# Residual stream parked in DRAM during the gate and up products, the final norm by halves of the tokens, and one mLSTM output projection placed earlier

## The chip, the cores and the metric

The kernel runs on one core of a Trainium2 chip. The metric is the device time of one execution in microseconds; the time of a kernel is the median of several executions. Within the kernel TensorE (PE) multiplies, PEld loads its weights, VectorE (DVE) and ScalarE (ACT) work on elements, GpSimd (POOL) does small work and issues accumulating transfers, and SyncE (SP) issues the other transfers in order.

## The reference

A trunk of two layers on 512 tokens with 1024 features, in float32:

```python
for layer in range(DEPTH):                       # DEPTH = 2
    x = x + 0.5 * swiglu(rmsnorm(x, ffn_norm[layer, 0]), ...)      # hidden size 2816
    h = rmsnorm(x, mix_norm[layer])
    y = mla(h, ...) if layer % 3 == 0 else mlstm(h, ...)           # 8 heads each
    x = x + y
    x = x + 0.5 * swiglu(rmsnorm(x, ffn_norm[layer, 1]), ...)
return rmsnorm(x, final_norm)
```

`swiglu` is `(silu(h @ w_gate) * (h @ w_up)) @ w_down`. So the phases are a gated block (f0), attention (a), two gated blocks (f1, f2), the matrix memory (m), a gated block (f3) and the final norm.

## The kernel before

**Data.** The residual x is kept transposed: eight tiles of 128 features by 512 tokens, in pairs, `xx[0]` to `xx[3]`, each 128x1024 float32 and in a pool of constants. All other large tiles (normed operands, activations, weights that are summed) come from one pool of 31 tiles of 128x1024 (`ARENA`, `duo`); plain weight pieces land in a pool of three (`wp`, tag `raw`).

**Products.** Every float32 product is three matmuls on operands split into a high and a low part: ACT casts the high part (`whi`, L162), DVE subtracts to get the low part (`wlo`, L163). A gated block does gate and up first: two plain pieces (`plain`, L411), then nine pieces by seven products instead of eight (`seven`, L433), 24 matmuls of 128x256 for each product. The operand combinations of the seven products are made from x by `normed_blocks` (L363). Down follows: `down_plain` (L507) and `down_seven` (L571), whose seven products end in additions into x (`add`, L599) and, for the next norm, squares of x on ACT that DVE sums (`square`, L261).

**Weights.** A list of planned pieces sets the order of the loads. SP issues them in that order (L122), four ahead of use; where two weight blocks have to be added, POOL issues the second as an accumulating transfer (L125, L167), or DVE adds (L150). An SP load into a buffer in use stands at the head of SP's queue until the buffer's last reader is done.

**The order of instructions** on each engine is fixed when the kernel is built, by a scheduler that goes by the order of the program and its own costs.

**mLSTM.** In `mlstm` (L947) the loop `for p in range(3)` (L1223) runs over pairs of heads. Per head, `conv` projects and convolves queries and keys, `gate` projects the output gate (`og`), `decay` makes the decay weights (spread of rows, exponentials on ACT into `dw`) and the scores `s`, `mix` multiplies scores and values (`num`) and sums rows (`rows`). `out(part, i)` is a piece of the output projection: 24 matmuls into `y` and two additions into x (L1265). In the last turn (p = 2) `out(0, 0)` stands behind `decay(6)`.

**Final norm.** `finish` (L1301) is called last: a sum over features by matmuls with ones (`st`, L273), the inverse root on POOL (L281), a spread over partitions by two matmuls with diagonal operands (`bc`, L292 and L296), then for each of the eight tiles of x one DVE instruction of 128x512 (L1306) and a transfer of 256 KB (L1308).

Of the kernel before, what the change touches and what calls it, by code (L numbers as in the profile page):

```python
# [34 lines left out]
P = 128  # L35
T = 512
# [6 lines left out]
NU = NF // 2  # L43
NB = 2
DC = 3
ARENA = 31
LOADS = 4
AHEAD = 2
WARM = 36
# [15 lines left out]
class Trunk:  # L65
    def __init__(self, ctx, tc, t, out):
        self.tc, self.nc, self.t, self.out = tc, tc.nc, t, out
        self.const = ctx.enter_context(tc.tile_pool(name="const", bufs=1))
        self.wp = ctx.enter_context(tc.tile_pool(name="wp", bufs=3))
        self.tmp = ctx.enter_context(tc.tile_pool(name="tmp", bufs=8))  # L70
        self.small = ctx.enter_context(tc.tile_pool(name="small", bufs=2))
        self.ps = ctx.enter_context(tc.tile_pool(name="ps", bufs=6, space=bass.MemoryType.PSUM))
        self.ps2 = ctx.enter_context(tc.tile_pool(name="ps2", bufs=2, space=bass.MemoryType.PSUM))
        self.arena = ctx.enter_context(tc.tile_pool(name="arena", bufs=ARENA))
        self.xx = [self.const.tile([P, 2, T], F32, name=f"xx{d}") for d in range(ND // 2)]
        self.x = [self.xx[d // 2][:, d % 2] for d in range(ND)]
        self.chunks, self.loads, self.loaded, self.split, self.made = [], [], [], [], {}
        self.first = 0

# [4 lines left out]
    def pair(self, name="pr"):  # L84
        d = self.duo(name)
        return d[:, :T], d[:, T:]

    def bank(self, name="mm"):
        return self.ps.tile([P, T], F32, name=name, tag="mm")
# [141 lines left out]
    def norm_begin(self, gcol):  # L231
        self.xg = [None] * ND
        self.gcol = gcol
        self.acc = self.small.tile([P, T], F32, name="acc", tag="acc", bufs=2)
        self.nacc = 0

    def norm_split(self, d):

# [1 line left out]
        self.split_to(self.xg[d], self.x[d], self.vec(self.gcol + d))  # L240

    def norm_square(self, d):
        self.square(self.acc, self.x[d], self.nacc == 0)
        self.nacc += 1

    def norm_tile(self, d):

# [4 lines left out]
    def norm_half(self, d, n):  # L252

        t = slice(n * T // 2, n * T // 2 + T // 2)
        if self.gcol is not None:
            if self.xg[d] is None:
                self.xg[d] = self.pair()
            self.split_to([a[:, t] for a in self.xg[d]], self.x[d][:, t], self.vec(self.gcol + d))
        self.square(self.acc[:, t], self.x[d][:, t], False)

    def square(self, acc, src, first):  # L261
        if first:
# [6 lines left out]
    def rstd(self, acc, n, times=None):  # L269

        st = self.ps2.tile([P, T], F32, name="st", tag="st")
        for q in range(NT):
            self.nc.tensor.matmul(st[:, q:q + 1], acc[:, q * P:(q + 1) * P], self.one, start=True, stop=True)  # L273
        ms = self.small.tile([P, NT], F32, name="ms", tag="ms")
        if times is not None:
            self.nc.vector.tensor_tensor(out=ms, in0=st[:, 0:NT], in1=times, op=ALU.mult)
            self.nc.vector.tensor_scalar(ms, ms, 1.0 / n, EPS, ALU.mult, ALU.add)
        else:
            self.nc.vector.tensor_scalar(ms, st[:, 0:NT], 1.0 / n, EPS, ALU.mult, ALU.add)
        r = self.small.tile([P, NT], F32, name="r", tag="r", bufs=6)  # L280
        self.nc.gpsimd.tensor_tensor(out=r, in0=ms, in1=self.mhalf[:, 0:NT], op=ALU.pow)  # L281
        return r

    def spread(self, r):

        hi = self.small.tile([P, NT], F32R, name="rh", tag="rh")
        lo = self.small.tile([P, NT], F32, name="rl", tag="rl")
        self.split_to((hi, lo), r)
        bc = self.ps2.tile([P, T], F32, name="bc", tag="st")
        for n, part in enumerate((hi.bitcast(F32), lo)):  # L290
            diag = self.tmp.tile([P, T], F32R, name="diag", tag="t")
            self.nc.vector.tensor_tensor(  # L292
                out=diag.rearrange("p (a b) -> p a b", a=NT),
                in0=self.ident[:, None, :].broadcast_to([P, NT, P]),
                in1=part[:, :, None].broadcast_to([P, NT, P]), op=ALU.mult)
            self.nc.tensor.matmul(bc, self.onesr, diag, start=n == 0, stop=n == 1)  # L296
        return bc

# [64 lines left out]
    def normed_blocks(self, rb):  # L363
# [35 lines left out]
        split(7, t3)  # L399
        yield  # L400
        b21 = block(1, 0)
        yield
        split(2, b21)
        yield
# [74 lines left out]
    def ffn(self, f, next_gain):  # L479
        v = self.nc.vector  # L480
        xg = self.xg
        self.gcol_now = self.gcol
        acts, slabs = [], []
        for j in range(NU):
            g, i = divmod(j - DC, 4)
            if j < DC:
                acts.append(self.duo("act", F32))
                outs = [acts[j][:, i * 256:i * 256 + 256] for i in range(4)]
            else:
                if i == 0:  # L490
                    slabs.append([self.duo("slab", F32) for _ in range(4)])
                outs = [a[:, i * 256:i * 256 + 256] for a in slabs[g]]
            if j < NB:
                for half in range(2):
                    self.plain(f, j, half, xg, acts[j][:, half * T:half * T + T])
            else:
                self.seven(outs)
            if i == 3 and j > DC:

                b11, b12, _, b22 = slabs[g]  # L500
                v.tensor_tensor(out=b12, in0=b22, in1=b12, op=ALU.subtract)
                v.tensor_tensor(out=b12, in0=b12, in1=b11, op=ALU.add)
        self.norm_begin(next_gain)
        self.down_plain(f, acts, self.operands(slabs))
        self.down_seven(slabs)
# [65 lines left out]
    def down_seven(self, slabs):  # L571
# [57 lines left out]
        for c in range(4):  # L629
            product(bw, 7, c, last=False)  # L630
            product(bx, 2, c)
        add(1, 1, bw, -0.5)
        add(0, 0, bx, 0.5)
        for d in range(4):
            self.norm_tile(d)
        for c in range(4):
            product(bw, 4, c, first=False)
            self.norm_half(4 + c, 1)
        add(1, 0, bw, -0.5)
        for d in range(4, 8):  # L640
            self.norm_half(d, 0)

    def plan_ffn(self, f):
        for j in range(NB):
# [302 lines left out]
    def mlstm(self, next_gain):  # L947
# [275 lines left out]
        for p in range(3):  # L1223
# [86 lines left out]
    def run(self, phases):  # L1310
        gains = {"f0": V_FFN, "f1": V_FFN + ND, "f2": V_FFN + 2 * ND, "f3": V_FFN + 3 * ND,
# [12 lines left out]
        for p, q in zip(phases, phases[1:] + ["end"]):  # L1324
# [3 lines left out]
                self.mla(gains[q])  # L1328
            else:
                self.mlstm(gains[q])  # L1330
        self.finish()

# [96 lines left out]
```

## Time and profile before

| | |
|---|---|
| median of 3 executions | 1866.14 us (1862.98 to 1870.06) |
| the profiled execution, its own time | 1857.42 us |
| its span in the trace | 1855.7 us |
| granted TensorE clock, mean of the span | 0.992 |
| PE busy | 1811.5 us (98%) |
| DVE, ACT, POOL busy | 79%, 50%, 7% |
| HBM read and written | 261.62 MB and 2.10 MB |

Durations in the trace belong to the profiled execution, which lies 8.7 us under the median. A row of a timeline gives the start in microseconds from the span's start, the duration, the engine, the line, the operation and, in brackets, how long the engine was idle before and what released it.

### The profile page before, as it was taken

How to read it: one execution, taken by the hardware profiler on the slowest of the kernel's cores; microseconds unless marked ns; L12 is line 12 of the kernel's file. 1: busy time of each engine (PE TensorE's matmuls, PEld its weight loads, DVE VectorE, ACT ScalarE, POOL GpSimd, SP SyncE). 2: the span in 40 equal slices, each digit the busy share in tenths (PEclk: the TensorE clock that was granted, in tenths of full speed). 3: DMA queues.
4: the chain of work that ended last, by engine and by line, in shares of the span. 5: the costliest groups of instructions: out<-in, count | busy, mean ns of one | idle time of the engine just before them, and what ended most of it. 6: DMA issues, size and time to landing. Idle time of an engine off the chain costs nothing.

```text
span 1855.7 us, 30086 instructions
## 1 busy us (share of the span) xinstructions
PE 1811.5 (98%) x12240; PEld 1662.8 (90%) x12240; DVE 1463.2 (79%) x1931; ACT 934.9 (50%) x1339; POOL 131.3 (7%) x154
## 2 busy tenths in 40 slices
PE   9999999999999999999999999999998999999996
PEld 7999989978887999989989999997876779999896
DVE  7877899777767877877796878778877778788875
ACT  5444545567544444544544444455757544445442
POOL 0010011000000010000001000100000000100010
PEclk9999999999999999999999999999998999999998
DMA  6683567421124684566377456733221246845662
GB/s 205 177 236 110 162 187 163 137 74 63 46 73 150 159 243 128 140 181 153 126 219 205 133 162 187 175 105 101 80 69 57 69 126 181 236 125 149 184 159 91
DMA packets 74906, 265.66 MB, mean 143 GB/s; under 512 B 8336, under 2 KB 9360, under 8 KB 74768
## 3 DMA queue, kind: packets, MB, share of 16 engines
q1 hardware_dynamic: 57312, 200.30, 30.9%
q0 software_dynamic: 17456, 63.44, 19.4%
q8 instruction: 96, 1.57, 0.3%
q14 instruction: 42, 0.34, 0.1%
HBM read 261.62 MB, written 2.10 MB: 142 GB/s over the span
## 4 chain that ended last, share of the span: by engine, by line
PE 73%; issue 13%; DVE 8%; ACT 3%; DMA 2%; POOL 0%; POOLq 0%; DVEq 0%; ACTq 0%
PE pz L450 4%; PE pw L449 4%; PE pw L448 4%; PE pz L449 4%; PE pz L448 4%; PE pw L450 3%; PE y L194 3%; PE y L196 3%; PE y L195 3%; PE px L449 3%; PE px L448 3%; PE px L450 3%; PE py L450 2%; DMA raw<-in_wgs 2%; PE py L448 2%
## 5 line engine op out<-in xcount | busy, mean ns | idle before, releaser
L162 ACT CAST whi<-raw 128x1024 fp32r<-128x1024 f32 (+1 forms) x278 | 284.9, 1025 | 412.2 <-issue 131.1
L163 DVE TENSOR_TENSOR wlo<-raw,whi 128x1024 fp32r<-128x1024 f32 (+1 forms) x278 | 330.5, 1190 | 109.1 <-ACT whi L162 108.1
L162 ACT CAST whi<-sum 128x1024 fp32r<-128x1024 f32 x208 | 217.5, 1047 | 278.5 <-PE pz L449 80.8
L163 DVE TENSOR_TENSOR wlo<-sum,whi 128x1024 fp32r<-128x1024 f32 x208 | 252.8, 1221 | 72.0 <-ACT whi L162 72.0
L150 DVE TENSOR_TENSOR sum<-raw,sum 128x1024 f32<-128x1024 f32 x88 | 107.2, 1219 | 25.6 <-DMA raw<-in_wgs 25.1
L125 POOL DMA_DIRECT2D sum<-in_wgs x72 | 61.6, 855 | 640.2 <-DMA sum<-in_wgs 278.3
L450 PE MATMUL py<-b6h,wlo 128*128 128x256 f32 x288 | 83.5, 290 | 10.6 <-DVE wlo L163 10.5
L448 PE MATMUL py<-b6h,whi 128*128 128x256 f32 x288 | 82.8, 288 | 2.2 <-ACT whi L162 2.2
L449 PE MATMUL py<-b6l,whi 128*128 128x256 f32 x288 | 82.4, 286 | 0.0
L450 PE MATMUL pz<-b5h,wlo 128*128 128x256 f32 x288 | 81.5, 283 | 0.8 <-DVE wlo L163 0.8
L450 PE MATMUL pw<-b7h,wlo 128*128 128x256 f32 x288 | 81.2, 282 | 0.0
L450 PE MATMUL px<-b2h,wlo 128*128 128x256 f32 x288 | 81.2, 282 | 0.0
L450 PE MATMUL pz<-b3h,wlo 128*128 128x256 f32 x288 | 81.2, 282 | 0.0
L450 PE MATMUL pw<-b4h,wlo 128*128 128x256 f32 x288 | 81.2, 282 | 0.0
L449 PE MATMUL pw<-b7l,whi 128*128 128x256 f32 x288 | 81.2, 282 | 0.0
L449 PE MATMUL pz<-b3l,whi 128*128 128x256 f32 x288 | 81.2, 282 | 0.0
L449 PE MATMUL px<-b2l,whi 128*128 128x256 f32 x288 | 81.2, 282 | 0.0
L449 PE MATMUL pw<-b4l,whi 128*128 128x256 f32 x288 | 81.2, 282 | 0.0
L450 PE MATMUL px<-b1h,wlo 128*128 128x256 f32 x288 | 81.2, 282 | 0.0
L449 PE MATMUL px<-b1l,whi 128*128 128x256 f32 x288 | 81.2, 282 | 0.0
L449 PE MATMUL pz<-b5l,whi 128*128 128x256 f32 x288 | 81.2, 282 | 0.0
L448 PE MATMUL px<-b1h,whi 128*128 128x256 f32 x288 | 81.2, 282 | 0.0
(418 smaller groups left out, 6137.1 us busy)
## 6 DMA issues: line engine op xcount, KB each, us to landing
raw<-in_wgs SPq DMA_DIRECT2D x108, 512.0 KB, 4.7
sum<-in_wgs SPq DMA_DIRECT2D x72, 512.0 KB, 6.8
sum<-in_wgs POOLq DMA_DIRECT2D x72, 512.0 KB, 7.2
sum<-in_wds POOLq DMA_DIRECT2D x48, 512.0 KB, 6.0
raw<-in_wds SPq DMA_DIRECT2D x48, 512.0 KB, 3.3
sum<-in_wds SPq DMA_DIRECT2D x32, 512.0 KB, 4.5
raw<-in_wgc SPq DMA_DIRECT2D x30, 512.0 KB, 3.3
raw<-in_wdn SPq DMA_DIRECT2D x24, 512.0 KB, 4.0
```

Of the source, the lines that this page charges most:

```text
L125: self.nc.gpsimd.dma_start(out=raw, in_=self.row(*plus), accum_op=ALU.add)
L150: self.nc.vector.tensor_tensor(out=t, in0=a, in1=b, op=ALU.add)
L162: self.nc.scalar.copy(out=hi[:, a:b], in_=raw[:, a:b])
L163: self.nc.vector.tensor_tensor(out=lo[:, a:b], in0=raw[:, a:b], in1=hi[:, a:b].bitcast(F32), op=ALU.subtract)
L194: mm(out, lhs[0], rhs[0], start=start, stop=False)
L195: mm(out, lhs[0], rhs[1], start=False, stop=False)
L196: mm(out, lhs[1], rhs[0], start=False, stop=stop)
L448: mm(out, wh, bh[:, b], start=first and e + k == 0, stop=False, skip_group_check=True)
L449: mm(out, wh, bl[:, b], start=False, stop=False, skip_group_check=True)
L450: mm(out, wl, bh[:, b], start=False, stop=last and e + k == 4, skip_group_check=True)
```

## The change

The pool of large tiles grows from 31 to 35, and x is taken from it as four tiles (`residual`). `normed_blocks` calls `leave` after its last read of x: four writes of 512 KB to DRAM on SP's queue. Before the down products of every gated block `come` takes four tiles again and reads them back on SP's queue. In `down_seven` of the last block (`gcol is None`) the second half of the tokens is normed as soon as its additions are done, ahead of the fourth product, and the first half at the end. `finish(n)` now does one half: ACT and POOL share the multiplications for all eight tiles of the second half and for two tiles of the first, DVE does six tiles of the first. In `mlstm` the projection `out(0, 0)` goes ahead of `decay(6)`.

```diff
-ARENA = 31
+ARENA = 35
-        self.xx = [self.const.tile([P, 2, T], F32, name=f"xx{d}") for d in range(ND // 2)]
-        self.x = [self.xx[d // 2][:, d % 2] for d in range(ND)]
+        self.dram = ctx.enter_context(tc.tile_pool(name="dram", bufs=2 * ND, space=bass.MemoryType.DRAM))
+        self.residual()
...
+    def residual(self):
+        self.xt = [self.duo("x", F32) for _ in range(ND // 2)]
+        self.xx = [a[:, :].rearrange("p (a b) -> p a b", a=2) for a in self.xt]
+        self.x = [self.xx[d // 2][:, d % 2] for d in range(ND)]
+    def leave(self):
+        self.away = []
+        for a in self.xt:
+            b = self.dram.tile([P, W], F32, name="away", tag="away")
+            self.nc.sync.dma_start(out=b, in_=a)
+            self.away.append(b)
+        self.x = None
+    def come(self):
+        self.residual()
+        for a, b in zip(self.xt, self.away):
+            self.nc.sync.dma_start(out=a, in_=b)
...
         b21 = block(1, 0)
+        self.leave()
...
+        self.come()
         self.norm_begin(next_gain)
         self.down_plain(f, acts, self.operands(slabs))
...
         add(1, 1, bw, -0.5)
+        if self.gcol is None:
+            for d in range(8):
+                self.norm_half(d, 1)
+            self.finish(1)
         add(0, 0, bx, 0.5)
         for d in range(4):
-            self.norm_tile(d)
+            self.norm_half(d, 0) if self.gcol is None else self.norm_tile(d)
         for c in range(4):
             product(bw, 4, c, first=False)
-            self.norm_half(4 + c, 1)
+            if self.gcol is not None:
+                self.norm_half(4 + c, 1)
         add(1, 0, bw, -0.5)
         for d in range(4, 8):
             self.norm_half(d, 0)
+        if self.gcol is None:
+            self.finish(0)
...
+            if p == 2:
+                out(0, 0)
             decay(a + 2)
-            conv(p + 2) if p < 2 else out(0, 0)
-            if p == 2:
+            if p < 2:
+                conv(p + 2)
+            else:
                 for f in pending:
                     f()
             decay(b + 2)
...
-    def finish(self):
+    def finish(self, n):
         nc = self.nc
-        rb = self.spread(self.rstd(self.acc, D))
+        t = slice(n * T // 2, n * T // 2 + T // 2)
+        bc = self.spread(self.rstd(self.acc, D, tiles=range(2 * n, 2 * n + 2)))
+        rb = self.small.tile([P, T], F32, name="rb", tag="rb", bufs=2)[:, :T // 2]
+        nc.scalar.copy(out=rb, in_=bc)
         for d in range(ND):
-            o = self.t512("o")
-            nc.vector.scalar_tensor_tensor(out=o, in0=self.x[d], scalar=self.vec(V_FIN + d), in1=rb,
-                                           op0=ALU.mult, op1=ALU.mult)
-            nc.sync.dma_start(out=self.out[d * P:(d + 1) * P, :], in_=o)
+            o = self.t512("o")[:, :T // 2]
+            gain = self.vec(V_FIN + d)
+            if n or d % 3 == 2:
+                nc.scalar.activation(o, self.x[d][:, t], AF.Identity, scale=gain)
+                nc.gpsimd.tensor_tensor(out=o, in0=o, in1=rb, op=ALU.mult)
+            else:
+                nc.vector.scalar_tensor_tensor(out=o, in0=self.x[d][:, t], scalar=gain, in1=bc,
+                                               op0=ALU.mult, op1=ALU.mult)
+            nc.sync.dma_start(out=self.out[d * P:(d + 1) * P, t], in_=o)
```

The scheduler moves instructions with it. Three places matter. The first is PE in the last turn of the mLSTM loop, around the scores `s` of head 6 (`qz` and `pr` are its operands). Before, with the last matmul of `num` of head 5 first and `y` of `out(0, 0)` last:

```order
L196 MATMUL num<-pr 128x128
L200 MATMUL rows<-pr,pick 128x512 x2
L200 MATMUL s<-qz,pr 128x512
L200 MATMUL s<-pr 128x512
L200 MATMUL s<-qz,pr 128x384
L200 MATMUL s<-pr 128x384
L200 MATMUL s<-qz,pr 128x256
L200 MATMUL s<-pr 128x256
L200 MATMUL s<-qz,pr 128x128
L200 MATMUL s<-pr 128x128
L194 MATMUL y<-pr,whi 128x512
```

Now, from the last three of the 24 matmuls into `y`:

```order
L214 MATMUL y<-pr,whi 128x512
L215 MATMUL y<-pr,whi 128x512
L216 MATMUL y<-pr,wlo 128x512
L1125 MATMUL spread<-pr,selr 128x512
L220 MATMUL s<-qz,pr 128x512
L220 MATMUL s<-pr 128x512
L220 MATMUL s<-qz,pr 128x384
L220 MATMUL s<-pr 128x384
L220 MATMUL s<-qz,pr 128x256
L220 MATMUL s<-pr 128x256
L220 MATMUL s<-qz,pr 128x128
L220 MATMUL s<-pr 128x128
```

All 24 matmuls into `y` now stand ahead of the scores, some of them between those of `num`, and the spread of head 6 moved from inside `num` to right ahead of its scores. The second place is ACT at the same point. Before, from the function of the last convolution (`conv`) to the first exponentials of head 6 (`dw`):

```order
L971 ACT_TABLE_LOAD
L971 ACTIVATE conv<-conv 128x512
L736 CAST pr<-conv 64x512 x2
L1115 ACT_TABLE_LOAD
L1115 ACTIVATE dw<-dg,cols 128x128
L206 CAST pr<-sq 128x512
L1139 ACT_TABLE_LOAD
L1139 ACTIVATE sg<-sg 128x512
L206 CAST pr<-sq 128x512
L1115 ACT_TABLE_LOAD
L1115 ACTIVATE dw<-spread,cols 128x128 x3
```

Now the same stretch:

```order
L1003 ACT_TABLE_LOAD
L1003 ACTIVATE conv<-conv 128x512
L182 CAST whi<-raw 128x1024
L768 CAST pr<-conv 64x512 x2
L1171 ACT_TABLE_LOAD
L1171 ACTIVATE sg<-sg 128x512
L226 CAST pr<-sq 128x512 x2
L1147 ACT_TABLE_LOAD
L1147 ACTIVATE dw<-dg,cols 128x128
L1147 ACTIVATE dw<-spread,cols 128x128 x3
```

One table load fell away, and the cast of a weight piece (`whi`), which waits for the last matmuls into `y` that read its buffer, now stands ahead of the casts of `conv`. The third place is ACT at the end of the program. Before:

```order
L266 ACTIVATE sq<-xx_78 128x256
L162 CAST whi<-raw 128x1024
L266 ACTIVATE sq<-xx_78 128x256
L266 ACTIVATE sq<-xx_79 128x256 x2
L266 ACTIVATE sq<-xx_78 128x256 x2
L266 ACTIVATE sq<-xx_79 128x256 x2
L206 CAST rh<-r 128x4
```

Now:

```order
L182 CAST whi<-raw 128x1024
L226 CAST rh<-r 128x2
L1348 ACTIVATE o<-x,par 128x256 x2
L1343 COPY rb<-bc 128x256
L1348 ACTIVATE o<-x,par 128x256 x6
L287 ACTIVATE sq<-x 128x256 x7
L226 CAST rh<-r 128x2
L1343 COPY rb<-bc 128x256
L1348 ACTIVATE o<-x,par 128x256 x2
```

The output tiles of the second half stand ahead of the last seven squares of the first. These squares and the two diagonal operands of the first half use the same eight buffers (`t512`) as the output tiles, so they wait for transfers of the second half to DRAM. On POOL the eight multiplications of the second half stand ahead of the inverse root of the first; on PE the `st` and `bc` matmuls of the second half stand after 27 and 48 of the 96 matmuls of the last product; on DVE the last two additions into x stand behind three sums of squares of the first half.

## Rows read from the trace of the kernel before

**Rows 1.** The page, part 1: busy microseconds of each engine, share of the span and number of instructions.

```profile
PE 1811.5 (98%) x12240; PEld 1662.8 (90%) x12240; DVE 1463.2 (79%) x1931; ACT 934.9 (50%) x1339; POOL 131.3 (7%) x154
```

**Rows 2.** Windows in the gate and up products of the four gated blocks; columns: stretch, length, busy time and count of PE, PEld, DVE, ACT, POOL, granted clock, DMA share, GB/s.

```profile
100.00:110.00 10.00, 10.00 (x86) 10.00 (x85) 9.18 (x11) 4.50 (x6) 1.71 (x2) 1.00 1.02 378
120.00:130.00 10.00, 7.55 (x51) 7.34 (x51) 9.27 (x11) 4.24 (x6) 0.85 (x1) 0.83 0.72 197
670.00:680.00 10.00, 7.67 (x52) 7.66 (x52) 9.13 (x12) 4.67 (x7) 0.85 (x1) 0.83 0.65 182
1010.00:1020.00 10.00, 8.30 (x69) 8.10 (x68) 5.03 (x8) 2.42 (x4) 0.85 (x1) 1.00 1.06 267
...
1600.00:1610.00 10.00, 7.86 (x63) 7.44 (x63) 6.95 (x9) 4.24 (x6) 0.00 (x0) 1.00 0.87 237
```

**Rows 3.** The chain of waits that ends in the PE wait at 123.6 us: start, duration, what.

```profile
110.42 1.23 DVE wlo L163
...
111.67 8.85 DMA raw<-in_wgs
...
120.61 1.23 DVE sum L150
...
122.43 1.15 DVE wlo L163
...
123.62 0.58 PE py L450
```

**Rows 4.** Timeline of PE in the last turn of the mLSTM loop: start, duration, engine, line, operation, shapes, count, idle time before it.

```profile
1414.94 0.50 PE L194 MATMUL num<-pr 128*128 128x512 f32 x1
...
1425.78 0.77 PE L200 MATMUL s<-qz,pr 128*128 128x512 f32 x1 [3.72 <-DVE pr L737]
...
1428.15 0.73 PE L194 MATMUL y<-pr,whi 128*128 128x512 f32 x1
...
1434.96 1.09 PE L200 MATMUL rows<-pr,pick 128*128 128x512 f32 x4
...
1437.33 0.45 PE L194 MATMUL og<-pr,whi 128*128 128x512 f32 x1
...
1442.97 0.40 PE L194 MATMUL num<-pr 128*128 128x512 f32 x1
...
1445.38 0.40 PE L194 MATMUL num<-pr 128*128 128x512 f32 x1
```

**Rows 5.** Windows of the same place, columns as in rows 2.

```profile
1410.00:1420.00 10.00, 8.12 (x39) 5.93 (x37) 7.94 (x15) 9.37 (x19) 0.00 (x0) 1.00 0.08 31
1420.00:1430.00 10.00, 5.29 (x15) 3.96 (x15) 8.27 (x12) 8.93 (x12) 0.00 (x0) 0.52 0.31 106
```

**Rows 6.** Timelines of ACT and DVE at the same place, columns as in rows 4.

```profile
1422.61 1.26 ACT L736 CAST pr<-conv 64x512 fp32r<-64x512 f32 x2
1423.89 1.28 ACT L1115 ACT_TABLE_LOAD   x1
...
1427.41 0.63 ACT L1139 ACTIVATE sg<-sg 128x512 f32<-128x512 f32 x1
...
1429.86 0.88 ACT L1115 ACTIVATE dw<-spread,cols 128x128 f32<-128x128 f32 x3
...
1421.79 1.40 DVE L1144 SCALAR_TENSOR_TENSOR sg<-sg,par,num 128x512 f32<-128x512 f32 x2
...
1423.70 1.21 DVE L163 TENSOR_TENSOR wlo<-raw,whi 128x1024 fp32r<-128x1024 f32 x1
1424.94 1.40 DVE L737 TENSOR_TENSOR pr<-conv,pr 64x512 fp32r<-64x512 f32 x2
...
1432.97 1.61 DVE L1118 SCALAR_TENSOR_TENSOR dw<-s,dw 128x512 f32<-128x512 f32 x3
```

**Rows 7.** Timeline of all engines at the end of the program.

```profile
1838.38 1.40 DVE L599 SCALAR_TENSOR_TENSOR xx<-dw,xx 128x512 f32<-128x512 f32 x2 [3.36 <-PE dw L591]
...
1838.78 0.28 PE L591 MATMUL dw<-b4h,wlo 128*128 128x256 f32 x1
1839.10 1.49 ACT L266 ACTIVATE sq<-xx 128x256 f32<-128x256 f32 x4 [6.33 <-DVE xx L599]
...
1841.84 1.02 PE L273 MATMUL st<-cst,acc 128*128 128x1 f32 x8 [2.79 <-DVE acc L267]
...
1843.15 1.03 POOL L281 TENSOR_TENSOR r<-ms,mhalf 128x4 f32<-128x4 f32 x1 [52.50 <-DVE ms L279]
...
1845.35 1.31 PE L296 MATMUL bc<-diag,onesr 128*128 128x512 f32 x2 [2.48 <-DVE diag L292]
...
1846.70 5.36 DVE L1306 SCALAR_TENSOR_TENSOR o<-xx,par,bc 128x512 f32<-128x512 f32 x8 [0.89 <-PE bc L296]
```

**Rows 8.** Groups of POOL's instructions, different shapes apart: line, engine, operation, shapes, count, then busy time, mean duration of one in ns, idle time before.

```profile
L1193 POOL TENSOR_TENSOR fp<-fc,mhalf 128x16 f32<-128x16 f32 x2 | 6.7, 3336 | 125.4 <-ACT fc L1192 125.4
L976 POOL MEMSET qz<- 64x512 f32 x8 | 4.2, 521 | 61.8 <-PE num L196 56.2 <-PE dy L591 5.2
```

**Rows 9.** The page, part 6: transfers, KB each, median us from issue to landing.

```profile
outT<-o SPq DMA_DIRECT2D x8, 256.0 KB, 2.2
```

**Rows 10.** Windows in the first pieces of f0 and ahead of its down products, columns as in rows 2.

```profile
55.00:60.00 5.00, 3.05 (x24) 2.64 (x22) 5.00 (x6) 2.08 (x4) 0.84 (x1) 1.00 0.97 177
...
210.00:215.00 5.00, 5.00 (x44) 5.00 (x44) 3.59 (x4) 2.76 (x3) 0.00 (x0) 1.00 0.01 3
```

More of the change, by code (lines that the diff above doesn't have):

```diff
@@ L234, in norm_begin @@
         self.acc = self.small.tile([P, T], F32, name="acc", tag="acc", bufs=2)
-        self.nacc = 0
+        self.nacc = [0, 0]
     def norm_split(self, d):
@@ L242, in norm_square @@
     def norm_square(self, d):
-        self.square(self.acc, self.x[d], self.nacc == 0)
-        self.nacc += 1
+        self.square(self.acc, self.x[d], self.nacc == [0, 0])
+        self.nacc = [n + 1 for n in self.nacc]
     def norm_tile(self, d):
@@ L258, in norm_half @@
             self.split_to([a[:, t] for a in self.xg[d]], self.x[d][:, t], self.vec(self.gcol + d))
-        self.square(self.acc[:, t], self.x[d][:, t], False)
+        self.square(self.acc[:, t], self.x[d][:, t], self.nacc[n] == 0)
+        self.nacc[n] += 1
     def square(self, acc, src, first):
@@ L267, in square, with rstd @@
             self.nc.vector.tensor_tensor(out=acc, in0=acc, in1=sq, op=ALU.add)
-    def rstd(self, acc, n, times=None):
+    def rstd(self, acc, n, times=None, tiles=range(NT)):
         st = self.ps2.tile([P, T], F32, name="st", tag="st")
-        for q in range(NT):
-            self.nc.tensor.matmul(st[:, q:q + 1], acc[:, q * P:(q + 1) * P], self.one, start=True, stop=True)
-        ms = self.small.tile([P, NT], F32, name="ms", tag="ms")
+        m = len(tiles)
+        for i, q in enumerate(tiles):
+            self.nc.tensor.matmul(st[:, i:i + 1], acc[:, q * P:(q + 1) * P], self.one, start=True, stop=True)
+        ms = self.small.tile([P, NT], F32, name="ms", tag="ms")[:, :m]
@@ L275, in rstd @@
         if times is not None:
-            self.nc.vector.tensor_tensor(out=ms, in0=st[:, 0:NT], in1=times, op=ALU.mult)
+            self.nc.vector.tensor_tensor(out=ms, in0=st[:, 0:m], in1=times, op=ALU.mult)
             self.nc.vector.tensor_scalar(ms, ms, 1.0 / n, EPS, ALU.mult, ALU.add)
         else:
-            self.nc.vector.tensor_scalar(ms, st[:, 0:NT], 1.0 / n, EPS, ALU.mult, ALU.add)
-        r = self.small.tile([P, NT], F32, name="r", tag="r", bufs=6)
-        self.nc.gpsimd.tensor_tensor(out=r, in0=ms, in1=self.mhalf[:, 0:NT], op=ALU.pow)
+            self.nc.vector.tensor_scalar(ms, st[:, 0:m], 1.0 / n, EPS, ALU.mult, ALU.add)
@@ L282, in rstd @@
+        r = self.small.tile([P, NT], F32, name="r", tag="r", bufs=6)[:, :m]
+        self.nc.gpsimd.tensor_tensor(out=r, in0=ms, in1=self.mhalf[:, 0:m], op=ALU.pow)
         return r
     def spread(self, r):
-        hi = self.small.tile([P, NT], F32R, name="rh", tag="rh")
-        lo = self.small.tile([P, NT], F32, name="rl", tag="rl")
+        m = r.shape[1]
+        hi = self.small.tile([P, NT], F32R, name="rh", tag="rh")[:, :m]
+        lo = self.small.tile([P, NT], F32, name="rl", tag="rl")[:, :m]
@@ L288, in spread @@
         self.split_to((hi, lo), r)
-        bc = self.ps2.tile([P, T], F32, name="bc", tag="st")
+        bc = self.ps2.tile([P, T], F32, name="bc", tag="st")[:, :m * P]
         for n, part in enumerate((hi.bitcast(F32), lo)):
-            diag = self.tmp.tile([P, T], F32R, name="diag", tag="t")
+            diag = self.tmp.tile([P, T], F32R, name="diag", tag="t")[:, :m * P]
             self.nc.vector.tensor_tensor(
-                out=diag.rearrange("p (a b) -> p a b", a=NT),
-                in0=self.ident[:, None, :].broadcast_to([P, NT, P]),
-                in1=part[:, :, None].broadcast_to([P, NT, P]), op=ALU.mult)
+                out=diag.rearrange("p (a b) -> p a b", a=m),
+                in0=self.ident[:, None, :].broadcast_to([P, m, P]),
+                in1=part[:, :, None].broadcast_to([P, m, P]), op=ALU.mult)
@@ L1330, in run @@
                 self.mlstm(gains[q])
-        self.finish()
 INV_FREQ = [
```

## The prediction

> **What bounds the kernel now.** The page's busy times come first: PE works 1811.5 us of a span of 1855.7 [rows 1], so a change can win only where PE waits, and I looked for these places with windows. In a full window of the seven products PE issues 86 matmuls of 128x256 in 10 us, 0.1165 us each [rows 2]. Each of the four gated blocks has one window with far fewer: 51, 52, 69 and 63 [rows 2]. The missing 35, 34, 17 and 23 matmuls are 109 x 0.1165 = 12.7 us. The chain of waits tells what stands there: a weight load is issued at 111.67, right after the DVE subtraction that frees its buffer, lands 8.85 us later, and DVE's sum, DVE's next subtraction and PE's `py` follow one after the other [rows 3]. The second place is the last turn of the mLSTM loop: between 1410 and 1430 PE issues 39 and 15 matmuls, and the granted clock falls to 0.52, which is mostly its lower level of 1.2 GHz [rows 5]; the scores of head 6 wait 3.72 us for DVE's operand [rows 4]. The third is the end: the last matmul of the last product starts at 1838.78, the span ends at 1855.7 [rows 7], and nothing covers these 17 us.
>
> **The change part by part.** The sum is made against the profiled execution, 1857.42 us; it lies 8.7 us under the median of 1866.14, and I carry the difference over to that.
>
> *Four more tiles in the pool: 0 (from -2 to +2).* In the order, several loads lose the wait for a pool buffer. The load of [rows 3], however, lands in the pool of three plain pieces and waits for the same DVE subtraction after the change as before; so it is in all four blocks. The loads that are freed stand either behind it in SP's queue, or move up by some 2 us into transfers that already fill the queues (DMA share 1.02, [rows 2]). The load still goes out at 111.67 and takes about 8.85 us. The bounds are what 0.5 us more or less of landing would make in four blocks.
>
> *Parking x: 0 (to +1).* Every block adds 2 MB of writes and 2 MB of reads. The writes go out while the plain pieces run. The reads are the one thing put ahead of something on SP's queue: the first piece of the down weights is behind them. At 210 to 215 the DMA share is 0.01 [rows 10], and the waits of the four reads end there, ahead of the DVE subtraction on which the weight piece waits anyway. At the 378 GB/s of [rows 2] 2 MB take 5.5 us. If this cover is gone, the down weights are late by up to that.
>
> *Start: +0.5 (from -1 to +2).* The new order loads the last two tiles of x behind four further weight pieces: 2 MB, 5.5 us at 378 GB/s. PE then does other plain pieces first. A loss of up to 2 us disappears at 55 to 60, where PE issues 24 matmuls where 43 fit and DVE is busy all 5 us [rows 10]: the 19 missing ones are 2.2 us.
>
> *The projection ahead of head 6: -4.6 (from -6.8 to 0).* Before, the 24 matmuls into `y` run from 1428.15 to 1434.96, 6.8 us, behind the waits [rows 4]; the whole of it is the most that can be won. Now they lie between `num` of head 5 (first matmul 1414.94) and the scores. The other eleven of `num` take 1.7 us, as behind 1442.97, and 24 at the 0.235 us of the output gate's (1437.33 to 1442.97, [rows 4]) take 5.6; with two short waits for operands, some 0.8, PE reaches the scores at about 1423.4. These come hardly earlier than before. ACT's weight cast, which waits for the last `y`, ends at about 1424.2; the two casts of the convolution take 1.26 [rows 6], to 1425.4. DVE has its two `sg` until 1423.2 [rows 6], then a subtraction (1.21), an addition into x and a product (0.65 each), and delivers the first operand at 1426.3, against 1425.78. The 16 matmuls of scores for heads 6 and 7 end at about 1429.5. **What is late next** is the output gate of head 7: its bank is free when DVE has multiplied the first scores with the decay weights. ACT needs 1425.4 + table 1.28 + sigmoid 0.63 + two casts 1.26 + table 1.28 + four exponentials 1.2 = 1431.0 [rows 6], DVE then 0.6, so 1431.6. From there 5.6 us, 0.8 for a part at the lower clock, and `num` of head 6 at 1438.0. It needs 1.9 and its row sums 0.9: `num` of head 7 at 1440.8, before at 1445.38 [rows 4]. That is 4.6. The lower bound is an output gate that runs at 1.2 GHz throughout: 5.6 us more, nothing won.
>
> *The end: -2.7 (from -4 to +3).* The last product's 96 matmuls begin at 1838.78 - 95 x 0.1165 = 1827.7. The second half's `st` comes after 27 of them, 1830.9, when its sums are just done; ones and mean 0.6, inverse root 1.03 [rows 7], casts and two diagonals of half size 1.2: `bc` at 1833.7, three matmuls late. For these waits and the four extra matmuls PE loses 0.8. At 1835.0 POOL can begin its eight multiplications of 128x256. Their length g has no row. The nearest is a memset of 512 columns, 0.52 us [rows 8]: 256 columns are 0.26, the lower bound; a product reads twice and writes once, so I take three such passes, 0.78. The far bound is POOL's longest two-operand row, 3.34 us [rows 8]. The Trainium skill's page "GPSIMD Engine Reference" (Performance versus the Vector engine) speaks against giving such work to GpSimd, which it has at half of VectorE's speed, with 4497 ns for an addition over 2048 columns. By it g would be an estimated 0.6, and the end 0.4 us better than with 0.78.
>
> With g = 0.78 the first two output tiles leave at 1836.6 and land 2.2 later [rows 9], 1838.8. Until then ACT's squares of the first half have no buffer. Three squares and sums later, 1839.9, DVE comes to the last additions into x, 1.5 later than at 1838.38 [rows 7]. From there to `st` is 3.46 as before, 1843.4. Two columns instead of eight take 0.3 instead of 1.02, the diagonals and the spread half: before, the first output started 4.86 after `st` [rows 7], now 3.2, at 1846.6. Six outputs of half size on DVE are 2.2, two on ACT and POOL 0.7 + 2g = 2.3, so 1848.9. Then 2.2 to land, 1.4 to the span's end (1855.7 - 1852.1 - 2.2, [rows 7, 9]) and 0.5 for SP's queue of transfers: 1853.0, 2.7 less. For a long g the inverse root waits behind eight multiplications, and the end is 1835.0 + 8g + 2.6 + 2g + 4.3 = 1841.9 + 10g: as before at g = 1.38.
>
> Sum: 0 + 0 + 0.5 - 4.6 - 2.7 = -6.8. The profiled execution would be 1850.6, the median **1859.3**.
>
> **Rivals.** *The pool was the cause of the four waits* (0.12). For it: they lie in the stretch where the freed loads are. Against it: the chain [rows 3] starts at a buffer of the other pool. If the landing came 3 us earlier, all 12.7 us go: 1846.6.
>
> *A sum on DVE waits for the multiplication under way on POOL* (0.16). The three sums of the first half ahead of the last additions into x have both operands in SBUF and run beside the eight multiplications; each would wait up to 0.78, and the additions come 2.3 later. The end wins 0.4, the kernel 4.5: 1861.6. The Trainium skill's page "SBUF — State Buffer" (Who interferes with whom) says that a VectorE instruction with two SBUF inputs and a GpSimd instruction that reads SBUF exclude each other for a whole instruction. No row before has the two together.
>
> *The mLSTM wait only changes its place* (0.10). The clock falls as before and the output gate runs slowly; the term is 0, and the sum -2.2: 1863.9.
>
> *Slower: the multiplications cost what POOL's other two-operand work costs* (0.10). On POOL the inverse root of the first half stands behind eight of them. At g = 3.34 the end is 1841.9 + 33.4 = 1875.3, 19.6 more, and with the other terms +15.5: 1881.6. It decides from g = 2.7 on, where the sum passes +9.3. For it: all of POOL's two-operand rows are 1 us and more, even with four columns [rows 7, 8]. Against it: they are powers, not products.
>
> **How the numbers follow.** My forecast has 0.52. Its terms allow -12 to +4. The range leaves out the slow multiplications and half of the first rival: 1848 to 1868. A measurement of this kernel can tell about 0.5% from no change, 9.3 us, that is 1856.8 and 1875.5. Faster by more: all of the first rival, 0.12, and two fifths of the forecast, 0.21: together 0.33. Slower by more: the last rival, 0.10. The rest, 0.57, is within.
>
> **What would show it.** In the new profile: windows of the four blocks with about 51, 52, 69 and 63 matmuls again, and the load still 8 to 9 us under way (else the first rival); `y` between 1415 and 1424, the scores at about 1426, the gate's first matmul some 2 us behind them, and `num` of head 7 at about 4.6 us less than before from `num` of head 5; on POOL eight multiplications of 0.6 to 0.9 us from 1835 on, and DVE's last additions into x 1 to 2 us behind the last matmul. The prediction is wrong if the multiplications take over 1.4 us, if sums on DVE are stretched beside them, or if PE waits ahead of the down products, where the reads of x stand in front of weights.

## The result and the profile after

The changed kernel takes 1874.66 us (median; 1872.39 to 1876.14). Against the kernel before the ratio is 1.0053, with an interval of 1.0035 to 1.0071: it is slower by 0.5%, 9.9 us. The two medians, of seven executions each, differ by 8.5. The forecast was 1859.3.

The two profiled executions differ by more, 18.6 us of span (1874.3 against 1855.7). The one of before was at the fast end of its kernel's executions (1857.42, the others 1858.97 to 1870.06). So sizes are taken from the runs below, and the trace says where to look.

The page, part 1, after:

```profile
PE 1820.1 (97%) x12242; PEld 1669.3 (89%) x12242; DVE 1459.8 (78%) x1936; ACT 937.8 (50%) x1355; POOL 142.4 (8%) x165
```

PE works some 9 us longer in a span that is 18.6 us longer [rows 1]. The windows below have the columns of [rows 2]. In each pair the first is the place of [rows 2], the second is the last gate/up piece but one of the same block (the eighth of nine; some of the expectations below call it the last).

```profile
120.00:130.00 10.00, 7.01 (x48) 6.81 (x48) 5.85 (x8) 3.19 (x5) 0.00 (x0) 0.86 1.05 308
205.00:215.00 10.00, 8.29 (x61) 8.08 (x60) 6.74 (x9) 3.19 (x5) 0.00 (x0) 0.88 0.63 220
...
675.00:685.00 10.00, 7.09 (x57) 6.68 (x56) 6.99 (x9) 4.24 (x6) 0.20 (x1) 1.00 1.03 313
760.00:770.00 10.00, 8.05 (x65) 7.64 (x64) 8.89 (x11) 4.24 (x6) 0.00 (x0) 1.00 0.54 205
1025.00:1035.00 10.00, 8.07 (x56) 7.87 (x55) 7.30 (x9) 3.39 (x6) 0.13 (x1) 0.84 1.04 313
1110.00:1120.00 10.00, 7.32 (x59) 6.90 (x59) 7.61 (x10) 4.24 (x6) 0.00 (x0) 1.00 0.49 182
1615.00:1625.00 10.00, 7.34 (x51) 7.13 (x50) 6.79 (x9) 3.19 (x5) 0.00 (x0) 0.87 1.01 310
1700.00:1710.00 10.00, 7.62 (x62) 7.21 (x61) 7.43 (x9) 4.24 (x6) 0.00 (x0) 1.00 0.51 193
```

The four old holes, windows in which PE issues far fewer than 86 matmuls, are still there: 48, 57, 56 and 51 matmuls. PE's four waits in them sum to 10.1 us, before to 8.2. And there are four new ones, 61, 65, 59 and 62 instead of 86. That is 97 missing, and 97 x 0.1165 = 11.3 us. Part 5 of the page shows the same in two groups, here before and then after:

```profile
L150 DVE TENSOR_TENSOR sum<-raw,sum 128x1024 f32<-128x1024 f32 x88 | 107.2, 1219 | 25.6 <-DMA raw<-in_wgs 25.1
...
L450 PE MATMUL py<-b6h,wlo 128*128 128x256 f32 x288 | 83.5, 290 | 10.6 <-DVE wlo L163 10.5
```

```profile
L170 DVE TENSOR_TENSOR sum<-raw,sum 128x1024 f32<-128x1024 f32 x88 | 107.3, 1219 | 45.3 <-DMA raw<-in_wgs 44.8
...
L474 PE MATMUL py<-b6h,wlo 128*128 128x256 f32 x288 | 85.8, 298 | 20.0 <-DVE wlo L183 19.9
```

DVE's sums now wait 45.3 us for a load, before 25.6; PE's `py` waits 20.0 us for `wlo`, before 10.6. The first new hole, in f0: PE, then DVE (start, duration, what, idle time before it).

```profile
209.28 0.28 PE L473 MATMUL py<-b6l,whi 128*128 128x256 f32 x1
211.28 0.39 PE L474 MATMUL py<-b6h,wlo 128*128 128x256 f32 x1 [1.71 <-DVE wlo L183]
```

```profile
203.15 0.41 DVE L479 TENSOR_TENSOR slab<-sg,px 128x256 f32<-128x256 f32 x1
208.26 1.23 DVE L170 TENSOR_TENSOR sum<-raw,sum 128x1024 f32<-128x1024 f32 x1 [4.70 <-DMA raw<-in_wgs]
209.41 0.68 DVE L497 TENSOR_TENSOR c<-u,pz 128x512 f32<-128x512 f32 x1
210.00 1.22 DVE L183 TENSOR_TENSOR wlo<-sum,whi 128x1024 fp32r<-128x1024 f32 x1
...
212.07 1.22 DVE L170 TENSOR_TENSOR sum<-raw,sum 128x1024 f32<-128x1024 f32 x1
```

It reads as "the load is late, so the sum is late, so `wlo` is late". That is wrong: the sum at 208.26 and the `wlo` at 210.00 belong to different pieces. The order of DVE's instructions, as built, with the buffers' numbers and the semaphores that each one waits for, tells it (cut at the dots). Before:

```
L473 TENSOR_TENSOR c12_2208<-u2_2043,pz_2013 128x512 [waits PE_49]
L163 TENSOR_TENSOR wlo_2216<-sum_2213,whi_2215 128x1024 [waits Activation_49]
L455 TENSOR_TENSOR slab_1772<-sg_2210,c12_2208 128x256 [waits Activation_49]
L150 TENSOR_TENSOR sum_2213<-raw_2146,sum_2213 128x1024 [waits DMAHW5_49,DVE_49]
...
L163 TENSOR_TENSOR wlo_2282<-sum_2080,whi_2281 128x1024 [waits DMASW1_49,PE_49,Activation_49]
L150 TENSOR_TENSOR sum_2448<-raw_2285,sum_2181 128x1024 [waits DMAHW0_49,DMASW2_49,DVE_49]
```

After:

```
L170 TENSOR_TENSOR sum_2458<-raw_2295,sum_2191 128x1024 [waits DMAHW5_49,DMASW2_49]
L497 TENSOR_TENSOR c12_2218<-u2_2053,pz_2023 128x512 [waits PE_49]
L183 TENSOR_TENSOR wlo_2226<-sum_2223,whi_2225 128x1024 [waits Activation_49]
L479 TENSOR_TENSOR slab_1782<-sg_2220,c12_2218 128x256 [waits Activation_49]
```

`sum_2458` (before `sum_2448`) is for product 6 of the next piece, the last one. Before, it stood eight instructions further down, behind the subtractions for products 6, 5 and 7 of the piece at hand, and one thing that it waited for was DVE itself (`DVE_49`): it took over the buffer of `sum_2080`, whose last reader is the subtraction into `wlo_2282` right ahead of it. With more buffers this wait is gone, and the scheduler puts the sum first. On the chip its load lands late; DVE stands 4.70 us, and `wlo_2226`, which PE needs now and which reads `sum_2223`, not `sum_2458`, stands behind it.

### The profile page after: what moved, and what is told of

Read it like the earlier page. It is cut to its first block, busy times and chain, and to the rows that moved or that the text cites. A ratio compares the mean times of both kernels' runs of the same rounds, so it can differ in the third digit from the quotient of the medians.

```text
span 1874.3 us, 30187 instructions
## 1 busy us (share of the span) xinstructions
PE 1820.1 (97%) x12242; PEld 1669.3 (89%) x12242; DVE 1459.8 (78%) x1936; ACT 937.8 (50%) x1355; POOL 142.4 (8%) x165
## 5 line engine op out<-in xcount | busy, mean ns | idle before, releaser
L183 DVE TENSOR_TENSOR wlo<-raw,whi 128x1024 fp32r<-128x1024 f32 (+1 forms) x278 | 330.4, 1191 | 106.5 <-ACT whi L182 106.2
L183 DVE TENSOR_TENSOR wlo<-sum,whi 128x1024 fp32r<-128x1024 f32 x208 | 252.8, 1222 | 72.5 <-ACT whi L182 72.3
L170 DVE TENSOR_TENSOR sum<-raw,sum 128x1024 f32<-128x1024 f32 x88 | 107.3, 1219 | 45.3 <-DMA raw<-in_wgs 44.8
L472 PE MATMUL pz<-b5h,whi 128*128 128x256 f32 x288 | 81.8, 284 | 0.0
L472 PE MATMUL pw<-b7h,whi 128*128 128x256 f32 x288 | 81.2, 282 | 0.0
L472 PE MATMUL px<-b2h,whi 128*128 128x256 f32 x288 | 81.2, 282 | 0.0
L472 PE MATMUL pz<-b3h,whi 128*128 128x256 f32 x288 | 81.2, 282 | 0.0
L472 PE MATMUL pw<-b4h,whi 128*128 128x256 f32 x288 | 81.2, 282 | 0.0
```

Source lines behind the costliest of these rows:

```text
L170: self.nc.vector.tensor_tensor(out=t, in0=a, in1=b, op=ALU.add)
L183: self.nc.vector.tensor_tensor(out=lo[:, a:b], in0=raw[:, a:b], in1=hi[:, a:b].bitcast(F32), op=ALU.subtract)
L472: mm(out, wh, bh[:, b], start=first and e + k == 0, stop=False, skip_group_check=True)
```

## The experiments

Three theories on the new holes were put to the test. **A:** the pool's relief lets loads out in a burst, and the one that matters lands late. **B:** the reads (or writes) of x make it late. **C**, formed after the first eight runs: the order on DVE, in which a sum that is not yet due stands ahead of a subtraction that is. Ratios are to the kernel before.

| run | ratio | interval |
|---|---|---|
| park_only | 1.0072 | 1.0059 to 1.0084 |
| mlstm_only | 0.9979 | 0.9968 to 0.9990 |
| tail_only | 0.9994 | 0.9984 to 1.0004 |
| keep_arena | 1.0007 | 0.9996 to 1.0018 |
| no_transfers | 1.0085 | 1.0066 to 1.0105 |
| late_reads | 1.0158 | 1.0134 to 1.0183 |
| keep_transfers | 1.0093 | 1.0071 to 1.0115 |
| loads3 | 1.0115 | 1.0093 to 1.0138 |
| pin_last | 0.9985 | 0.9973 to 0.9997 |
| pin_all | 0.9886 | 0.9869 to 0.9904 |
| before_pinned | 0.9916 | 0.9901 to 0.9932 |
| best_pinned | 0.9896 | 0.9879 to 0.9913 |

**The parts one by one.** Each is one part of the change on the kernel before.

```diff
 # park_only
-ARENA = 31
+ARENA = 35
+        self.residual()
...
+        self.leave()
...
+        self.come()
```

> Before plus the parking of x alone: four more tiles in the pool, x written to DRAM in the second plain pieces and read back ahead of the down products; mLSTM loop and end as before. Theory from the two traces: the parking is the whole loss, and more than the 18.6 us by which the profiled span grew, since the other two parts win a little. Start +1.4 to +3.0, one new wait of PE in the last gate/up piece of each of the four gated blocks (py waits for DVE's wlo, this for the sum, this for the load of raw) at 2.2 to 3.0 us each with the stretch at the lower clock, the rest of the shift spread over the down products: +20 to +22 us, ratio about 1.011. Rival, the prediction's terms: +0.5 for parking and start, and the loss lies in the other parts: ratio 1.000, no new wait in the last pieces.

+13.4 us, less than the traces of the first pair had suggested, and enough for all of the loss. The four new holes are in its trace too: PE's waits there are 1.6, 1.6, 2.4 and 1.9 us, in the changed kernel 1.7, 1.5, 2.3 and 2.0.

```diff
 # mlstm_only
+            if p == 2:
+                out(0, 0)
             decay(a + 2)
-            conv(p + 2) if p < 2 else out(0, 0)
```

> Before plus the moved mLSTM projection alone. The prediction: num of head 7 4.6 us earlier from num of head 5, and all of it kept: -4.6. From the trace of after: about 4 us won up to num of head 7, then two new waits of PE (1.85 us ahead of the transposes into ab, 1.25 behind), since the factors now stand at the end of a chain ACT, DVE, PE that runs no earlier: -1.5 to -2.5. Rival: the wait only changes place: 0 (+-0.5).

-3.9 us (-6.0 to -1.9): a gain, between the two expectations.

`tail_only` has the diffs of `down_seven`, `rstd`, `spread` and `finish`, with the counters that they need, and no others.

> Before plus the end in halves of the tokens alone. The prediction: -2.7. From the trace of after: multiplications on POOL of 0.77 us, but DVE's sums beside them 0.80 instead of 0.42 and the squares late for want of buffers: -1.1. Rival: the end has no part in it, 0 (+-0.5).

-1.1 us (-3.0 to +0.7): not told apart from nothing.

```diff
 # keep_arena: park_only, without
-        self.leave()
-        self.come()
```

> x in four tiles of a pool of 35, kept there for the whole kernel, so that 31 tiles are left for the rest as before; nothing is written out or read back; mLSTM loop and end as before. It changes only how x is first loaded: tiles are written whole, and the order of x among the first weights is the one of after. Theory: the start of after (+1.4 by 23.5 us, +3.0 by 63 us) comes from this order: +1.4 to +3.0, and no new wait in the last gate/up pieces. Rival: the start comes from the parking (writes of x on the same queue), then this one is as before: 0 (+-0.5).

+1.3 us (-0.7 to +3.4), no new hole. The three parts add up within their intervals: 13.4 - 3.9 - 1.1 = 8.4, against 9.9 measured (6.5 to 13.2).

**What in the parking costs.**

```diff
 # no_transfers: in leave and come
-            self.nc.sync.dma_start(out=b, in_=a)
-            self.nc.sync.dma_start(out=a, in_=b)
+            self.nc.gpsimd.memset(a, 0.0)
```

> The parking without its transfers: the four tiles of x go back to the pool as in the change, but nothing is written out, and new tiles of zeros (GpSimd) stand for x behind the gate and up products, so the rest is computed on other numbers. mLSTM loop and end as before. Theory A (the relief of the pool): loads of the last gate/up piece that before waited for a pool buffer go out in a burst, with three accumulating ones among them, and the load of raw that DVE's sum needs shares the queues with them: the new wait of PE stands in all four blocks, some 2.5 us each, so +10 to +13 against before, ratio 1.006, as parking alone (1.0072). Theory B (the transfers): the reads of x right behind that load, or the writes, make the wait: no new wait, and the time that of x kept in the pool, ratio 1.000 to 1.002.

```diff
 # late_reads: park_only, with the reads in down_plain
-        self.come()
+                if h == 0 and c == 1:
+                    self.come()
```

> Parking alone, with the reads of x moved behind the second piece of the down weights, some 10 us later in the program; the writes stay, and mLSTM loop and end are as before. Theory A (relief of the pool): the new waits in the last gate/up pieces stay, 2 to 3 us each, ratio 1.006 to 1.008. Theory B (reads): the waits are gone, ratio 1.000 to 1.002. If the reads share the blame, the load of raw comes down from the 8.1 us of after to a value between that and the 6.2 us of before, and the waits are about half.

Theory B falls twice. Without any transfer of x the loss is 15.8 us, and the four new holes stand in the trace, with waits of 1.5, 1.7, 2.1 and 1.7 us. With the reads moved away the new holes stay; they even grow, to waits of 3.1, 3.2, 3.9 and 3.6 us. The loss of late_reads, 29.4 us, is far over what A had forecast as well: from the first down product of f0 to the attention's first matmul another 4.8 us go (120.1 us, in park_only 115.3), of which 0.9 is a wait behind the addition into x; the rest was not followed up. In late_reads the load has no read of x near it and takes 8.0 us all the same. Waits of late_reads between 203 and 215 us (who waits for whom, us in total, times, longest):

```profile
DVE sum L170 <- DMA raw<-in_wgs: 4.6, 1, 4.6
PEld py L471 <- DVE wlo L183: 3.3, 1, 3.3
```

```diff
 # keep_transfers: park_only, read back into the same tiles
     def come(self):
-        self.residual()
```

> x stays in its four tiles (31 others are left, as before), but the 2 MB of writes and 2 MB of reads are made in each gated block, back into the same tiles; with nothing to wait for, the reads go out early, among the loads of the first gate/up pieces. Mlstm loop and end as before. Theory A (relief): no new wait in the last pieces; the time is that of x kept in the pool (1.0007), plus at most 0.5 to 1 us a block where transfers delay the first pieces: ratio 1.000 to 1.003. Theory B in its form on writes and traffic: the 4 MB a block cost by themselves 5 us or more, ratio over 1.004.

No new hole in the last pieces, as A has it, but 17.3 us lost: A's ratio is missed, and B's for the traffic (over 1.004) is met. A good part is lost at another place than the new holes. With nothing to wait for, the reads go out among the loads of the plain pieces, and the first pieces by seven products wait longer. PE there, in keep_transfers and then in keep_arena:

```profile
62.29 0.58 PE L467 MATMUL py<-b6h,whi 128*128 128x256 f32 x1 [3.41 <-ACT whi L180]
```

```profile
60.12 0.39 PE L453 MATMUL py<-b6h,whi 128*128 128x256 f32 x1 [1.63 <-ACT whi L167]
```

By part 5 of the two pages PE's waits at `py` for `whi` are 11.2 us against 2.2, those for `wlo` 10.0 against 12.3: 6.7 of the 13.9 us between the two spans; the rest was not followed up. DVE's first sum comes 2.2 us later in keep_transfers without any idle time ahead of it: by the two timelines of DVE it stands there behind the last `gr`, `ur` and `act` of the plain pieces, of 0.7 us each, and in keep_arena ahead of them. So this run says nothing on transfers placed as in the change.

```diff
 # loads3: the changed kernel
-LOADS = 4
+LOADS = 3
```

> The changed kernel with at most three loads ahead of their use where it had four. Theory A (relief: a burst of loads): the pace comes back, the load of raw that the last gate/up piece waits for goes out with fewer beside it, its 8.1 us fall to some 6.5 and the four new waits shrink from 2.5 us to under 1: 6 to 10 us less than the changed kernel, ratio to before 0.998 to 1.002. Theory B (reads of x): they still stand where they stood, and the ratio stays at 1.005. A loss elsewhere is possible for both, where a load that is issued later lands too late; then other waits on raw appear.

Slower than the changed kernel by 0.6%. The waits mostly move: those at `py` for `wlo` fall to 5.6 us, but PE waits 2.4 to 3.5 us twice in a block at `pz` (product 3), 22.1 us in all, since accumulating loads are now late. Part 5 of its page:

```profile
L170 DVE TENSOR_TENSOR sum<-raw,sum 128x1024 f32<-128x1024 f32 x88 | 107.4, 1221 | 65.2 <-DMA sum<-in_wgs 45.0
```

Up to here A was the theory that fitted the places of the new holes, but it had forecast the times of the last three runs wrongly. DVE's order, above, gave theory C.

**The order held.** `issue_after` queues an instruction behind a given one on its engine, and adds no wait for anything else. Against the changed kernel, pin_last and pin_all change the order on DVE and, by one place in each block, one cast on ACT; against the kernel before, before_pinned changes the order on DVE alone. PE, GpSimd and SP keep theirs.

```diff
 # pin_last: the changed kernel; in value()
-            self.nc.vector.tensor_tensor(out=t, in0=a, in1=b, op=ALU.add)
+            if n[0] == "gu" and len(n) == 3 and n[2] == NU - NB - 1:
+                with self.tc.issue_after(self.los[-5].ins):
+                    self.nc.vector.tensor_tensor(out=t, in0=a, in1=b, op=ALU.add)
+            else:
+                self.nc.vector.tensor_tensor(out=t, in0=a, in1=b, op=ALU.add)
```

`los` lists the subtractions of L183. pin_all (on the changed kernel), before_pinned (on the kernel before) and best_pinned (before, with the mLSTM and end parts) have `n[2] > 0` in place of the last condition. In before_pinned this moves two sums a block by eight places each.

> The changed kernel, with one place in DVE's order held: in the last gate/up piece of each block the sum for its product 6 is issued behind the fifth subtraction before it, where it stood before the change; the change had moved it ahead of the subtraction that PE waits for. Nothing else is touched, and the load goes out as in the changed kernel. Theory C (order): PE's wait was never for this sum; the subtraction it needs stood behind it in DVE's queue while the sum waited for a load that is not yet due. The four new waits are gone, 10 to 11 us less than the changed kernel, ratio to before 0.998 to 1.001; the four old waits stay. Theory A (the load itself is late, by the burst): the sum is as late as before and PE waits as long, at the same place or one product on: ratio 1.004 to 1.006.

By the ratios 12.7 us less than the changed kernel, give or take 4, and now faster than before. DVE at the same place in pin_last:

```profile
201.84 0.69 DVE L502 TENSOR_TENSOR c<-u,pz 128x512 f32<-128x512 f32 x1
202.86 1.23 DVE L188 TENSOR_TENSOR wlo<-sum,whi 128x1024 fp32r<-128x1024 f32 x1 [0.33 <-ACT whi L187]
...
208.61 1.23 DVE L188 TENSOR_TENSOR wlo<-sum,whi 128x1024 fp32r<-128x1024 f32 x1 [0.99 <-ACT whi L187]
209.76 1.22 DVE L173 TENSOR_TENSOR sum<-raw,sum 128x1024 f32<-128x1024 f32 x1
```

The sum runs at 209.76, with no idle time; `wlo` runs at 202.86. The load that it waits for is as slow as in the changed kernel. The two plain loads of this stretch, in the changed kernel and in pin_last:

```profile
DMA to landing us min/median/max: 6.8/7.5/8.1
```

```profile
DMA to landing us min/median/max: 6.7/7.5/8.3
```

The slower one, 8.1 and 8.3, is the sum's. So the load is late, as theory A has it, and that costs nothing by itself: PE's windows are full. Windows of pin_last, the old hole of f0 and the places of the four new ones:

```profile
120.00:130.00 10.00, 7.62 (x51) 7.41 (x50) 7.59 (x10) 3.42 (x6) 0.64 (x1) 0.83 1.01 307
203.00:213.00 10.00, 10.00 (x86) 10.00 (x85) 8.73 (x10) 4.20 (x6) 0.00 (x0) 1.00 0.93 333
...
755.00:765.00 10.00, 10.00 (x85) 10.00 (x85) 8.09 (x10) 5.26 (x7) 0.00 (x0) 1.00 0.68 263
...
1105.00:1115.00 10.00, 10.00 (x86) 10.00 (x85) 8.27 (x9) 5.35 (x7) 0.00 (x0) 1.00 0.58 213
...
1690.00:1700.00 10.00, 10.00 (x86) 10.00 (x85) 7.99 (x10) 5.00 (x6) 0.00 (x0) 1.00 0.60 235
```

> The changed kernel, with the sum for product 6 held behind the fifth subtraction before it in every gate/up piece but the first. Theory C: the four waits that the kernel before had are of the same making (there too a sum of the next piece stands seven subtractions too early), so both sets go: 10 to 11 us and the 12.7 us of the windows, 20 to 24 less than the changed kernel, ratio to before 0.991 to 0.994. Theory A: the waits of before stay, since their weight load takes 8.85 us whatever the order; ratio not under 0.998.

> The kernel before with the same hold in every gate/up piece but the first, and nothing of the change. Theory C: the four waits (2.67, 2.55, 1.92 and 1.97 us on PE, 12.7 us with the lower clock behind them) are gone: ratio 0.993 to 0.995. Theory A: as before, 0.999 to 1.001.

> The kernel before with the moved mLSTM projection and the end in halves, without the parking, and with the same hold in DVE's order. If the parts add up: mLSTM 0.9979, end 0.9994, hold by theory C 0.993 to 0.995: together 0.990 to 0.992, some 1846 us. By theory A 0.997.

The old holes are of the same making. In the order of before, at the place of [rows 3], `sum_1499` for product 6 of the next piece stands two ahead of `wlo_1266`, which reads `sum_1263`; the sum at 120.61 waited 5.72 us for its load. before_pinned has nothing of the change and is 0.84% faster, 15.7 us (12.7 to 18.5). Old places in pin_all, then `py` in before_pinned, whose waits fall from 10.6 to 2.4 us:

```profile
118.00:128.00 10.00, 10.00 (x85) 10.00 (x84) 8.36 (x11) 4.21 (x6) 0.00 (x0) 1.00 1.04 304
...
663.00:673.00 10.00, 10.00 (x85) 10.00 (x85) 8.46 (x10) 4.07 (x6) 0.68 (x1) 1.00 1.05 304
...
1010.00:1020.00 10.00, 10.00 (x86) 10.00 (x85) 7.38 (x9) 4.46 (x5) 1.17 (x2) 1.00 0.93 274
...
1590.00:1600.00 10.00, 10.00 (x85) 10.00 (x85) 7.98 (x9) 4.08 (x6) 0.86 (x1) 1.00 0.99 288
```

```profile
L455 PE MATMUL py<-b6h,wlo 128*128 128x256 f32 x288 | 81.7, 284 | 2.4 <-DVE wlo L168 2.3
```

pin_all (1842.45 us) and best_pinned (1844.70) beat both kernels; their intervals overlap, so the parking brings nothing that can be told, even with the order held. C's forecasts of these runs held in their sign and came out too small: pin_all gained more than its 0.991 to 0.994 by more than its interval, and before_pinned and best_pinned lie past the good end of theirs by less than the interval. Where the surplus comes from was not followed up.

## Why the prediction was wrong

**The step that failed** is "four more tiles in the pool: 0 (from -2 to +2)". It measured +12.7: so much the changed kernel loses by the place of one sum a block (pin_last against it). The parking as a whole measured +13.4, and it takes no transfer of x for that (no_transfers). I followed the freed loads in SP's order, and bounded the term by landings of half a microsecond. But a freed buffer also frees the instruction that writes into it. The sum on DVE lost its wait for a buffer and was placed ahead of work that PE needed. I had the order of DVE before me and did not read it at this place. The range was not wide enough for its own terms either: their bounds add up to -13.8 to +8.0, not to the "-12 to +4" that is given. Even +8.0 would have ended at 1874.1, short of the 1874.66 measured.

**The root was a reading of [rows 3].** "DVE's sum, DVE's next subtraction and PE's `py` follow one after another" is true of the times, and I took it for a line of operands. The sum there is of the next piece as well; the subtraction only stood behind it in the queue. Read beside the buffers' numbers, the rows would have shown a gain of some 12.7 us for the taking, and that the sum's place is what a freed buffer can move. The first rival had the price, but by a wrong mechanism: more buffers did not bring the 12.7 us, they doubled the holes.

The Trainium skill's page "Perfetto Trace Analysis" (Optimization Strategy) has it that the same gap repeating on the engine that should be full can mean too few buffers for the next tile. Here it was not so: the gap repeats in all four blocks, four more buffers added a second one, and an order held with 31 buffers removed it (0.9916).

**Parking x: 0 to +1, and the start: +0.5.** With the order held, the change measures -2.8 us (pin_last, -5.0 to -0.6). Its other parts are -3.9 and -1.1, and keep_arena +1.3, so writes and reads of x, with what the relief does besides the order, add some 0.9 us, less than these runs can tell from nothing. The start is in keep_arena's +1.3. Nothing measured speaks against either term; neither is told apart from 0.

**The mLSTM projection: -4.6.** Right in its mechanism, and near in size: -3.9 (-6.0 to -1.9). PE in mlstm_only:

```profile
1417.74 0.39 PE L194 MATMUL y<-pr,whi 128*128 128x512 f32 x1
...
1428.84 0.47 PE L200 MATMUL s<-qz,pr 128*128 128x512 f32 x1 [2.64 <-DVE pr L737]
...
1434.22 0.56 PE L194 MATMUL og<-pr,whi 128*128 128x512 f32 x1 [0.60 <-DVE dw L1118]
...
1444.08 0.40 PE L194 MATMUL num<-pr 128*128 128x512 f32 x1
...
1454.65 0.38 PE L1009 MATMUL ab<-cst,a 8*128 8x8 f32 x4 [1.53 <-DVE a L1185]
```

Here `num` of head 5 starts at 1417.40, 2.46 later than in [rows 4]. With that taken off, the scores come at 1426.4 (forecast 1426.3), the output gate at 1431.8 (1431.6), `num` of head 7 at 1441.6 (1440.8): 3.8 us won there. Some of it goes back in a place that the prediction did not look at: the transposes into `ab` now wait for DVE's factors, and come 3.1 us earlier.

**The end: -2.7.** It measured -1.1 (-3.0 to +0.7), which alone does not speak against -2.7. By the traces, from the last product's first matmul to the span's end, it won 0.6 in tail_only and 1.1 in the changed kernel. The multiplication was sized well: 0.77 us against 0.78. What failed is the row behind it. POOL, DVE and ACT at the end of the changed kernel:

```profile
1855.04 6.16 POOL L1349 TENSOR_TENSOR o<-o,rb 128x256 f32<-128x256 f32 x8 [2.09 <-ACT rb L1343]
```

```profile
1858.06 0.80 DVE L288 TENSOR_TENSOR acc<-acc,sq 128x256 f32<-128x256 f32 x1 [4.02 <-ACT sq L287]
1859.02 1.59 DVE L288 TENSOR_TENSOR acc<-acc,sq 128x256 f32<-128x256 f32 x2 [0.17 <-ACT sq L287]
1860.54 1.27 DVE L624 SCALAR_TENSOR_TENSOR x<-dw,x 128x512 f32<-128x512 f32 x2
1861.75 2.01 DVE L288 TENSOR_TENSOR acc<-acc,sq 128x256 f32<-128x256 f32 x4
```

```profile
1857.60 0.42 ACT L287 ACTIVATE sq<-x 128x256 f32<-128x256 f32 x1 [0.24 <-DMA outT<-o]
1858.57 0.73 ACT L287 ACTIVATE sq<-x 128x256 f32<-128x256 f32 x2 [0.55 <-POOL o L1349]
```

The three sums beside POOL's multiplications take 0.80 us each, the four in a row behind them 0.50. That is the second rival, at some 0.9 us instead of the 2.3 that it was given; two buffers that come late add 0.8.

**The other rivals.** "The multiplications cost 3.34" is refuted by 0.77. "The mLSTM wait only changes its place" is refuted by 0.9979. The mechanism of the outcome was not among those that I had: the only slower case was at the end of the program.

## What to carry to other kernels

Where a scheduler or a list fixes the order, ask of a freed buffer which instruction it lets move, on every engine, and what then stands behind it. A chain of waits shows who came next on an engine, not who needed whom: check by the buffers' numbers whether the waiting instruction reads what the one ahead wrote. If it does not, holding the one ahead back in the order may be worth more than any transfer, here 0.84% for two sums a block, on the kernel as it was.

## What the runs showed of the hardware

A sum of 128x256 on DVE with both operands in SBUF takes 0.80 us beside GpSimd's multiplications, 0.50 in a row of four behind them. The Trainium skill's page "SBUF — State Buffer" (SBUF: two separate sides) has such a pair exclude each other for a whole instruction. The trace agrees that the sum is hindered; a wait for a whole multiplication would be up to 0.77 us, and 0.30 is what was seen. Executions of one unchanged kernel spread from 1858.0 to 1870.4 us, more than any of the parts here but the order: two single traces compared would have put the loss at 18.6 us instead of 9.9.
